# A hybrid decoder layer on one core: a fourth accumulator bank, gated operand loads, and one weight tile prepared earlier

## The chip, the cores and the metric

The kernel runs on one core of a Trainium2 chip. A core has TensorE (PE, matrix products, with its weight loads shown as PEld), VectorE (DVE), ScalarE (ACT), GpSimd (POOL) and SyncE (SP, here the queue that issues most transfers). The metric is device time in microseconds (us) of one launch, lower is better. "x3" behind a row stands for three instructions, L1631 for line 1631 of the kernel before.

## The reference

One layer of a decoder with four mixers side by side, for one prompt of 1024 positions and 8 samples of 8 positions (1088 tokens in all), model width 1024, in fp32:

```python
h = rmsnorm(x, norm_mix_pre[l])
(a_b, a_c, a_u, b_p, c_q, c_f, c_i, c_g, d_a, d_g) = jnp.split(h @ w_in[l], N_BLOCKS, axis=-1)
... # four mixers: ya, yb, yc, yd, 256 columns each
mix = jnp.concatenate([ya, yb, yc, yd], axis=-1) @ w_out[l]
x = x + rmsnorm(mix, norm_mix_post[l])
h = rmsnorm(x, norm_ffn_pre[l])
ff = (jax.nn.silu(h @ w_gate[l]) * (h @ w_up[l])) @ w_down[l]
x = x + rmsnorm(ff, norm_ffn_post[l])
```

The hidden width of the last part is 2816, 22 blocks of 128. The change touches how the products with `w_out`, with `w_gate` and `w_up`, and with `w_down` are fed; it changes none of them.

## The kernel before

Everything lies transposed: 128 features on the partitions, tokens along a row. Each fp32 operand is kept as two parts, a high one that ACT makes by a cast (CAST) and a low one that DVE makes by a subtract (`TT`, line 65, prints as TENSOR_TENSOR). A product is then three matmuls: high x high, high x low, low x high. So each weight tile needs a load, a cast and a subtract before PE can use all of it: `split2k` does the last two for a tile of 128x512.

The stages in order of time in the profiled execution:

1. to 335 us: norm of the input, the product with `w_in` (L997) in units of 128 columns, and the mixers between them. A planner (`hook`, `fill`, `drive`) gives DVE and PE their order here: at each group of matmuls it takes steps from three lists, `first`, `crit` and, when these have nothing, `bulk`. Their order on these two engines is then the order in which they were written. The last two units are 14 and 15; behind unit 15 a gate (`c_g`) multiplies the results `ys[4]` and `ys[5]` by silu(z).
2. 335 to 440 us: `project`, the product with `w_out` (L1131). Its right operands are the high and low parts `XH[k]`, `XL[k]` of the mixers' results, made by `put_y` in the order `korder` = (6, 7, 2, 3, 0, 1, 4, 5), and PE goes through k in that order. Its weights are `WO[n]`, for each of 8 output tiles two half tiles, h = 0 for k of 0 to 3 and h = 1 for k of 4 to 7. `out_steps` loads, casts and subtracts one `WO[n]`.
3. 440 to 925 us: the hidden units. Most go through `strassen(i, pr)` (L1403, from 518 us): two blocks of tokens and two of hidden features with 7 products of 12 matmuls each in place of 8. `pr` counts two pairs of token pieces, and `together` runs both in step: one product of pr 0, one of pr 1. The 7 products go into PSUM banks: b11 into a; t2 into b; t1 into c; b21 onto a; t3 onto b; t4 onto b; b22 onto c. Between them DVE reads sums out of the banks. PSUM has 8 banks, and the two in step use 6.
4. 925 to 1094 us: the down projection `down2` (L1631), again 7 products a step, in 4 groups g of 4 steps j. The right operands of group g are 14 tiles of 128x1088, from DRAM (`hx`): for g = 0 loaded and split on the chip, for the others loaded ready by POOL's queue (`x_item`, 42 loads). Free places for them are kept in `room`: 23 places, of which 14 are in use by a group; in the last step of a group each product frees two. `xs.step()` takes the next load in hand. The sums go to `acc` and `accp`; ACT copies (L1642, L1651) or DVE adds.
5. to 1181 us: the rest of the down projection (L1513), the last norm and the output.

From `down2` on the orders of PE, DVE, ACT and POOL are those in which the instructions are written. In stage 3 a scheduler orders them.

Of the kernel before, what the change touches and what calls it, by code (L numbers as in the profile page):

```python
# [17 lines left out]
P = 128  # L18
# [34 lines left out]
def body(ctx, tc, xn, xT, win, wout, wgu, wdn, par, con, msk, poolw, s_conv, s_pool, s_hgrn, s_conf,  # L53
# [330 lines left out]
    def chain(*gens):  # L384
        for g in gens:
            yield from g
# [636 lines left out]
    def out_steps(pools):  # L1023
        n = len(WO)
        WO.append([wop(pools) for h in range(2)])
        raws = [raw2k() for h in range(2)]
        for h in range(2):
            SY.dma_start(raws[h].rearrange("p (k c) -> p k c", c=P), wout[n][:, h * 4:h * 4 + 4])
        for h in range(2):
            yield 0.6  # L1030
            split2k(raws[h], WO[n][h])

# [16 lines left out]
    with tc.manual_schedule(engines={mybir.EngineType.PE, mybir.EngineType.DVE}):  # L1049
        for i, n in enumerate(UNITS):  # L1050
            handler, j = HANDLERS[n]
            nxt = UNITS[i + 1] if i + 1 < len(UNITS) else None
            if n in pu:
                first.append(handler(j, pu[n]))
                if i == 1:
                    until(lambda: free["mm"] >= 3)
                continue
            until(lambda: n in wq and len(wq[n]) == 2 and free["mm"] >= 3)
            give(mm=-3)
            ps = mm3()  # L1060
            if nxt is not None:
                load_unit(nxt)
                first.append(chain(wait(3), prep_steps(nxt)))
            else:
                bulk.insert(0, put_y())
            drive(unit(n, ps))
            del wq[n]
            first.append(handler(j, ps))
        bulk.insert(0, chain(out_steps([(wp, 4)]), out_steps([(wp, 4)])))
        until(lambda: not first and not crit and not bulk)  # L1070
    ph1.close()
    ph12.close()
# [315 lines left out]
    quads = {}  # L1388

    def strassen(i, pr):  # L1390
        a, b, c = bank(), bank(), bank()
        if i >= 2 * NPAIR:
            hst = T(w3, [P, 2, PW], "hst", bufs=2)
        else:
            if i % 2 == 0:
                quads[pr] = T(px, [P, 4, PW], "x")
            hst = quads[pr][:, 2 * (i % 2):2 * (i % 2) + 2]

        def prod(ps, wop, name, first):
            x = xop(name, pr)  # L1400
            for kk in range(4):
                for wi, xi in ((0, 0), (0, 1), (1, 0)):
                    PE.matmul(ps[:, :PW], wop[:, wi, kk * P:(kk + 1) * P], x(kk, xi),  # L1403
                              start=first and kk == 0 and wi == 0 and xi == 0, stop=kk == 3 and wi == 1,
                              skip_group_check=True)

        def buf(tag):
            return T(w3, [P, PW], tag, bufs=2)

        a11, s2, s1, a12, s3, a22, s4 = hid[i]  # L1410
        prod(a, a11, "b11", True)
        p1 = buf("p1")
        S.copy(p1, a[:, :PW])
        yield
        prod(b, s2, "t2", True)
        u2 = buf("u2")
        TT(u2, b[:, :PW], p1, ALU.add)
        yield
        prod(c, s1, "t1", True)
        yield  # L1420
        prod(a, a12, "b21", False)
        g0 = buf("g0")
        S.activation(g0, a[:, :PW], AF.Silu)
        yield
        prod(b, s3, "t3", False)
        c22 = buf("c22")
        TT(c22, b[:, :PW], p1, ALU.add)
        TT(c22, c[:, :PW], c22, ALU.add)
        yield
        prod(b, a22, "t4", False)  # L1430
        TT(p1, b[:, :PW], p1, ALU.add)
        yield
        prod(c, s4, "b22", False)
        TT(u2, c[:, :PW], u2, ALU.add)
        S.activation(u2, u2, AF.Silu)
        oa, ob = PIECES[2 * pr], PIECES[2 * pr + 1]
        TT(hst[:, 0], g0, p1)
        TT(hst[:, 1], u2, c22)
        if i >= 2 * NPAIR:
            SY.dma_start(hd[i][:, oa:oa + PW], hst[:, 0])  # L1440
            SY.dma_start(hd[i][:, ob:ob + PW], hst[:, 1])
        elif i % 2:
            pair_sums(i // 2, pr)
        yield
# [96 lines left out]
    def x_item(g, e):  # L1541

        p, name = 2 * g + e % 2, OPS[e // 2]
        src = hx[p][OPS.index(name)]

        def begin():
            if g:
                return None
            raw = T(w4, [P, 2 * PW], "raw", bufs=3).rearrange("p (q c) -> p q c", c=PW)
            SY.dma_start(raw, src[:, :2 * PW].rearrange("p (q c) -> p q c", c=PW))  # L1550
            return raw

        def work(raw):
            i, t = take()
            if g:
                GP.dma_start(t, src.bitcast(F32R))
            t = t.rearrange("p (w q c) -> p w q c", w=2, q=2)
            if not g:
                S.copy(t[:, 0], raw)
                TT(t[:, 1], raw, f32(t[:, 0]), ALU.subtract, eng=V if e % 2 else GP)  # L1560
            xop2[p, name] = t, i

        return begin, work

    def h_items(k):

        def item(c):
            o, n = DC[c]

            def begin():  # L1570
                raw = T(w4, [P, 2 * PW], "raw", bufs=3)[:, :n]
                SY.dma_start(raw, hd[k][:, o:o + n])
                return raw

            def work(raw):
                if c == 0:
                    hops[k] = [take()[1] for _ in range(2)]
                hi, lo = (h[:, o:o + n] for h in hops[k])
                S.copy(hi, raw)
                TT(lo, raw, f32(hi), ALU.subtract, eng=GP)  # L1580

            return begin, work

        return [item(c) for c in range(len(DC))]


    def load_ws(g, j):
# [35 lines left out]
    def down2(g, j, pr, ws, accp):  # L1623
        a, b, c = bank(), bank(), bank()
        oa, ob = PIECES[2 * pr], PIECES[2 * pr + 1]

        def prod(ps, name, first):
            for q in range(2):
                x = xop2[2 * g + q, name][0]
                for wi, xi in ((0, 0), (0, 1), (1, 0)):  # L1630
                    PE.matmul(ps[:, :PW], ws[name][wi][q], x[:, xi, pr], start=first and q == 0 and wi == 0 and xi == 0,  # L1631
                              stop=q == 1 and wi == 1, skip_group_check=True)

        def add(jj, o, ps):
            y = acc[jj][:, o:o + PW]
            TT(y, ps[:, :PW], y, ALU.add)

        y = accp[pr][:, j]
        prod(a, "b11", True)
        yield  # L1640
        if g == 0:
            S.copy(y, a[:, :PW])  # L1642
        else:
            TT(y, a[:, :PW], y, ALU.add)
        for ps, name, first, jj, o in ((b, "t2", True, j, ob), (c, "t1", True, j + NQ, ob), (a, "b21", False, j, oa),
                                       (b, "t3", False, j + NQ, ob), (c, "b22", False, j, ob), (b, "t4", False, j + NQ, oa)):
            prod(ps, name, first)
            yield
            y = acc[jj][:, o:o + PW]
            if g == 0 and name not in ("t3", "b22"):  # L1650
                S.copy(y, ps[:, :PW])  # L1651
            else:
                TT(y, ps[:, :PW], y, ALU.add)
# [41 lines left out]
    with tc.manual_schedule(engines={mybir.EngineType.Activation, mybir.EngineType.DVE, mybir.EngineType.PE, mybir.EngineType.Pool}):  # L1695
        for i, (g, j) in enumerate(order):
            wst.step()
            gens = [down2(g, j, pr, wsp[i], accp) for pr in range(2)]
            for e in range(8):
                for gen in gens:  # L1700
                    next(gen, None)
                if j == NQ - 1 and e < 7:
                    room += [xop2[2 * g + q, OPS[e]][1] for q in range(2)]
                if prep:
                    next(prep[0], None)
                if i == 0 and e < 2:
                    xs.step()
                elif i > 0 and e % 2 == 0 or j == NQ - 1 and e > 2:
                    if room and (xs.items or xs.raws):
                        xs.step()  # L1710
                if g == NGP - 1:
                    if e % 2 and (room[1:] or len(hs.items) % 3 != 1):
                        hs.step()
                    if e == 7:
                        add_p1(j + NQ, 0, GP if j < NQ - 1 else V)
                if i == len(order) - 1 and e in (0, 4, 1, 5):
                    if e < 4:
                        wraw.append(start_wd(e, 0))
                    else:
                        wds[e - 4, 0] = split_wd(e - 4, wraw.pop(0), (wp, 4) if e > 4 else None)  # L1720
            del prep[:]
# [165 lines left out]
```

## Time and profile before

| | us |
|---|---|
| median of three runs | 1183.06 (1183.0 to 1186.05) |
| profiled execution | 1182.58 |
| its span | 1180.8 |
| PE busy | 1145.0 (97%) |
| DVE busy | 881.4 (75%) |
| ACT busy | 455.5 (39%) |
| POOL busy | 96.8 (8%) |
| mean granted clock of PE | 0.995 |

The span goes from the first to the last instruction; the launch takes 1.78 us more. A row of a timeline gives start, duration, engine, line, operation, output<-inputs, and in brackets how long the engine was idle before and what ended that. A row of a table of waits gives who waited for whom, us in all, how often, and the longest. Granted clock is PE's share of its full speed.

### The profile page before, as it was taken

Reading aid. Unit: us, or ns where it says so; the run is one execution under the profiler, and the core shown is the slowest. Engines: PE = TensorE matmul, PEld = TensorE weight load, DVE = VectorE, ACT = ScalarE, POOL = GpSimd, SP = SyncE. Lnnn points to the kernel's source line nnn. Section 1 sums busy time; section 2 is a strip of 40 time slices with the busy share of each in tenths; the row PEclk is TensorE's granted clock in tenths of the full one; section 3 lists DMA queues with packets and bytes.
Section 4 is the critical chain, followed back from the end, with each engine's and each line's share of the span. In section 5 each row is a group of like instructions: output and inputs, shape, how many; then the busy total and the mean of one; then the engine's idle time right before and its main releaser. Section 6 shows DMA issues by size and latency. Waiting matters only on the chain.

```text
span 1180.8 us, 21827 instructions
## 1 busy us (share of the span) xinstructions
PE 1145.0 (97%) x8480; PEld 1111.1 (94%) x8480; DVE 881.4 (75%) x1831; ACT 455.5 (39%) x1006; POOL 96.8 (8%) x132
## 2 busy tenths in 40 slices
PE   5999999999999999999999999999999999999995
PEld 4899899998999999999999999999999999999995
DVE  5478979997674678786667787787676568888676
ACT  7535322253364453442333444444343442123321
POOL 2000000000000000000000000000000320127323
PEclk9999999999999999999999999999999999999998
DMA  7011112211145123022331542453454965843555
GB/s 264 30 42 24 37 38 69 41 37 29 41 157 176 39 75 129 24 80 79 112 112 50 186 162 95 162 170 111 140 182 125 297 207 180 298 159 105 168 101 105
DMA packets 103401, 136.91 MB, mean 116 GB/s; under 512 B 25025, under 2 KB 72257, under 8 KB 103297
## 3 DMA queue, kind: packets, MB, share of 16 engines
q1 hardware_dynamic: 94944, 108.71, 29.3%
q0 software_dynamic: 8352, 26.81, 7.8%
q8 instruction: 66, 1.08, 0.4%
q14 instruction: 39, 0.31, 0.1%
HBM read 94.90 MB, written 40.57 MB: 115 GB/s over the span
## 4 chain that ended last, share of the span: by engine, by line
PE 84%; DVE 5%; DMA 4%; issue 2%; ACT 2%; POOL 1%; SPq 0%; DVEq 0%; ACTq 0%; POOLq 0%
PE p L1403 27%; PE mm L997 16%; PE p L1631 14%; PE p L1131 8%; PE p L1513 6%; PE p L1312 5%; PE mm L148 2%; PE sm L811 1%; DVE wop L65 1%; DMA raw<-wgu 1%; DMA hx<-hi 1%; DVE raw L65 1%; DMA y<-xn 1%; DMA raw<-hx 1%; PE sm L886 1%
## 5 line engine op out<-in xcount | busy, mean ns | idle before, releaser
L65 DVE TENSOR_TENSOR wop<-raw,wop 128x512 fp32r<-128x512 f32 (+2 forms) x296 | 196.1, 675 | 105.3 <-ACT wop L1020 95.0
L1020 ACT CAST wop<-raw 128x512 fp32r<-128x512 f32 (+1 forms) x240 | 142.5, 604 | 252.0 <-DVE raw L65 115.7
L1403 PE MATMUL p<-xh,wop 128*128 128x272 f32 x1216 | 235.1, 288 | 0.0
L1403 PEld LDWEIGHTS p<-xh,wop 128*128 128x128 f32 x1216 | 193.3, 188 | 0.0
L1403 PE MATMUL p<-t,wop 128*128 128x272 f32 x912 | 179.3, 288 | 5.2 <-DVE c L65 5.2
L1403 PE MATMUL p<-xl,wop 128*128 128x272 f32 x608 | 175.6, 289 | 0.0
L997 PE MATMUL mm<-xh,wop 128*128 128x256 f32 (+2 forms) x864 | 175.3, 331 | 0.0
L1403 PEld LDWEIGHTS p<-t,wop 128*128 128x128 f32 x912 | 145.6, 188 | 6.5 <-DVE c L65 6.5
L997 PEld LDWEIGHTS mm<-xh,wop 128*128 128x128 f32 x864 | 137.4, 188 | 6.0 <-issue 1.1
L1403 PE MATMUL p<-x,wop 128*128 128x272 f32 x456 | 131.0, 287 | 0.0
L1403 PEld LDWEIGHTS p<-xl,wop 128*128 128x128 f32 x608 | 114.4, 188 | 0.0
L1131 PE MATMUL p<-xh,wop 128*128 128x272 f32 x512 | 100.6, 293 | 2.0 <-DVE wop L65 2.0
L997 PE MATMUL mm<-xl,wop 128*128 128x256 f32 (+2 forms) x432 | 97.3, 333 | 0.0
L1403 PEld LDWEIGHTS p<-x,wop 128*128 128x128 f32 x456 | 86.0, 189 | 0.0
L1131 PEld LDWEIGHTS p<-xh,wop 128*128 128x128 f32 x512 | 82.2, 191 | 2.2 <-DVE wop L65 2.2
L1631 PE MATMUL p<-xh,wop 128*128 128x272 f32 x456 | 81.6, 287 | 1.1 <-ACT x L1642 1.1
L1631 PE MATMUL p<-xl,wop 128*128 128x272 f32 x456 | 81.0, 287 | 0.0
L65 DVE TENSOR_TENSOR raw<-raw,raw 128x512 f32<-128x512 f32 (+1 forms) x123 | 71.2, 589 | 9.6 <-DMA raw<-wgu 8.1
L71 DVE SCALAR_TENSOR_TENSOR y<-u,taps,y 128x1024 f32<-128x1024 f32 x60 | 77.0, 1284 | 1.6
L1131 PE MATMUL p<-xl,wop 128*128 128x272 f32 x256 | 74.5, 291 | 0.0
L1312 PE MATMUL p<-xh,wop 128*128 128x272 f32 x384 | 74.1, 289 | 0.0
L997 PEld LDWEIGHTS mm<-xl,wop 128*128 128x128 f32 x432 | 69.2, 188 | 3.3 <-issue 0.8
(322 smaller groups left out, 1972.9 us busy)
## 6 DMA issues: line engine op xcount, KB each, us to landing
raw<-wgu SPq DMA_DIRECT2D x88, 256.0 KB, 3.0
hx<-hi SPq DMA_DIRECT2D x84, 136.0 KB, 2.1
raw<-win SPq DMA_DIRECT2D x40, 256.0 KB, 2.9
hx<-x SPq DMA_DIRECT2D x64, 136.0 KB, 2.5
raw<-wdn SPq DMA_DIRECT2D x32, 256.0 KB, 3.8
xh<-hx POOLq DMA_DIRECT2D x15, 544.0 KB, 9.8
xl<-hx POOLq DMA_DIRECT2D x15, 544.0 KB, 10.7
x<-hx POOLq DMA_DIRECT2D x12, 544.0 KB, 9.7
```

The costliest lines, as they stand in the source:

```text
L65: (eng or V).tensor_tensor(out, a, b, op)
L71: (eng or V).scalar_tensor_tensor(out=out, in0=a, scalar=s, in1=b, op0=op0, op1=op1)
L148: PE.matmul(ps[c][:, :n], hl[:, wi, kk], X[k][:, o:o + n], start=k == 0 and wi == 0 and X is XH, stop=k == KT - 1 and wi == 1)
L811: PE.matmul(ps[:rows, g * P:(g + 1) * P], kk[:, o:o + rows], qz[hf][:, :, g * 64:(g + 1) * 64], start=True, stop=True, skip_group_check=True)
L886: PE.matmul(op[hs, :gn], v[:gn, g, hs], attn[:gn, g, h, :gn], start=True, stop=g == 0, skip_group_check=True)
L997: PE.matmul(ps[c][:, :w], hl[:, wi, kk], X[k][:, o:o + w], start=k == order[0] and wi == 0 and X is XH, stop=k == order[-1] and wi == 1)
L1020: S.copy(hl[:, 0], raw)
L1131: PE.matmul(ps[nt][:, :PW], WO[nt][k // 4][:, wi, kk:kk + P], X[k][:, o:o + PW], start=k == korder[0] and wi == 0 and X is XH, stop=k == k ...
L1312: PE.matmul(ps[r][:, :PW], w[:, wi, (k % 4) * P:(k % 4 + 1) * P], X[k][:, o:o + PW], start=k == 0 and wi == 0 and X is XH, stop=k == KT - ...
L1403: PE.matmul(ps[:, :PW], wop[:, wi, kk * P:(kk + 1) * P], x(kk, xi), start=first and kk == 0 and wi == 0 and xi == 0, stop=kk == 3 and wi == 1,
L1513: PE.matmul(ps[:, :n], wd[:, wi, kk * P:(kk + 1) * P], hops[k][xi][:, o:o + n], start=first and kk == 0 and wi == 0 and xi == 0, stop=not ...
L1631: PE.matmul(ps[:, :PW], ws[name][wi][q], x[:, xi, pr], start=first and q == 0 and wi == 0 and xi == 0, stop=q == 1 and wi == 1, skip_group ...
```

## The change

Three edits.

First, in `strassen`, a fourth bank d. The product t4 starts in d and no longer continues in b. The sums are regrouped: t3 and p1 from b go into p1, then c and p1 into c22, and later d and p1 into p1. There are three sums as before. All 8 banks are then in use.

```diff
-        a, b, c = bank(), bank(), bank()
+        a, b, c, d = (bank() for _ in range(4))
...
         prod(b, s3, "t3", False)
+        TT(p1, b[:, :PW], p1, ALU.add)
         c22 = buf("c22")
-        TT(c22, b[:, :PW], p1, ALU.add)
-        TT(c22, c[:, :PW], c22, ALU.add)
+        TT(c22, c[:, :PW], p1, ALU.add)
         yield
-        prod(b, a22, "t4", False)
-        TT(p1, b[:, :PW], p1, ALU.add)
+        prod(d, a22, "t4", True)
+        TT(p1, d[:, :PW], p1, ALU.add)
```

Second, in the down projection, each of the 42 ready loads is preceded on POOL by a one-column add that reads the sum written last (`mark`), so that the load isn't issued before that sum. Which products take a load in hand changes too: in steps 0 to 2 of a group products 0, 3 and 6 (with the very first step of all, products 3 and 6), where it was 0, 2, 4 and 6 (and none in the first step). In step 3 it is 0 and 2 to 7; before, in groups 1 to 3, the same.

```diff
             if g:
+                if mark:
+                    TT(gate1, mark[0], mark[0], ALU.add, eng=GP)
                 GP.dma_start(t, src.bitcast(F32R))
...
+    mark = []
+    gate1 = T(const, [P, 1], "gate")
...
             y = acc[jj][:, o:o + PW]
+            mark[:] = [y[:, :1]]
...
-                elif i > 0 and e % 2 == 0 or j == NQ - 1 and e > 2:
+                elif e % 3 == 0 if j < NQ - 1 else e != 1:
```

Third, `WO[0]` is prepared ahead of `put_y`, where it and `WO[1]` were prepared behind it; and each `WO[n]` is split with h = 1 first.

```diff
-        for h in range(2):
+        for h in (1, 0):
             yield 0.6
             split2k(raws[h], WO[n][h])
...
-                bulk.insert(0, put_y())
+                bulk.insert(0, chain(out_steps([(wp, 4)]), put_y()))
...
-        bulk.insert(0, chain(out_steps([(wp, 4)]), out_steps([(wp, 4)])))
+        bulk.insert(0, out_steps([(wp, 4)]))
```

DVE between the mixers and `project`, before. `wop` is a half tile of weights (3141 and 3142 are `WO[0]`, 3154 and 3155 `WO[1]`), `xl` a low part (20 and 21 are k = 6 and 7, 16 and 17 k = 2 and 3, 14 and 15 k = 0 and 1, 18 and 19 k = 4 and 5), `y_27` is the gated `ys[5]`.

```order
L65 TENSOR_TENSOR y_26_106<-y_26_106,z_3048 128x448
L65 TENSOR_TENSOR xl_20_94<-y_28_108,xh_12_86 128x1088
...
L65 TENSOR_TENSOR xl_15_89<-y_23_103,xh_7_81 128x1088
L65 TENSOR_TENSOR wop_3141<-raw_3143,wop_3141 128x512
L65 TENSOR_TENSOR y_27_107<-y_27_107,z_3137 128x256
L65 TENSOR_TENSOR y_27_107<-y_27_107,z_3137 128x384
L65 TENSOR_TENSOR y_27_107<-y_27_107,z_3137 128x448
L65 TENSOR_TENSOR wop_3142<-raw_3144,wop_3142 128x512
L65 TENSOR_TENSOR wop_3154<-raw_3156,wop_3154 128x512
L65 TENSOR_TENSOR wop_3155<-raw_3157,wop_3155 128x512
L65 TENSOR_TENSOR xl_18_92<-y_26_106,xh_10_84 128x1088
```

The same place after. 3053 and 3052 are now `WO[0]`, h = 1 and h = 0; 3152 and 3151 are `WO[1]`.

```order
L65 TENSOR_TENSOR y_26_106<-y_26_106,z_3048 128x448
L65 TENSOR_TENSOR wop_3053<-raw_3055,wop_3053 128x512
L65 TENSOR_TENSOR wop_3052<-raw_3054,wop_3052 128x512
L65 TENSOR_TENSOR xl_20_94<-y_28_108,xh_12_86 128x1088
...
L65 TENSOR_TENSOR xl_15_89<-y_23_103,xh_7_81 128x1088
L65 TENSOR_TENSOR wop_3152<-raw_3154,wop_3152 128x512
L65 TENSOR_TENSOR y_27_107<-y_27_107,z_3147 128x256
L65 TENSOR_TENSOR y_27_107<-y_27_107,z_3147 128x384
L65 TENSOR_TENSOR y_27_107<-y_27_107,z_3147 128x448
L65 TENSOR_TENSOR wop_3151<-raw_3153,wop_3151 128x512
L65 TENSOR_TENSOR xl_18_92<-y_26_106,xh_10_84 128x1088
```

Two subtracts moved from behind k = 1 and y to ahead of k = 6, and two in place of four now stand between y_26's low part (k = 4) and those before it.

DVE in the next-to-last hidden unit (about 896 us), before: `c` is c22, `p` on the right a bank (10015 is b and 10016 c of pr 0, 10033 and 10034 those of pr 1) or p1 (1278, 1283), `raw` and `wop` the next units' weights.

```order
L65 TENSOR_TENSOR c_1288_10142<-p_10015,p_1278_10030 128x272
L65 TENSOR_TENSOR raw_10257<-raw_10256,raw_10257 128x2x128
L65 TENSOR_TENSOR c_1288_10142<-p_10016,c_1288_10142 128x272
L65 TENSOR_TENSOR c_1289_10157<-p_10033,p_1283_10048 128x272
L65 TENSOR_TENSOR c_1289_10157<-p_10034,c_1289_10157 128x272
L65 TENSOR_TENSOR wop_10480<-raw_10256,wop_10480 128x512
L65 TENSOR_TENSOR p_1278_10030<-p_10015,p_1278_10030 128x272
```

After, at the same rows (10050, 10051 and 10052 are b, c and d of pr 0; 10069 and 10070 b and c of pr 1; 1314 and 1320 are p1):

```order
L65 TENSOR_TENSOR p_1314_10066<-p_10050,p_1314_10066 128x272
L65 TENSOR_TENSOR raw_10294<-raw_10293,raw_10294 128x2x128
L65 TENSOR_TENSOR c_1325_10180<-p_10051,p_1314_10066 128x272
L65 TENSOR_TENSOR p_1320_10085<-p_10069,p_1320_10085 128x272
L65 TENSOR_TENSOR c_1326_10195<-p_10070,p_1320_10085 128x272
L65 TENSOR_TENSOR wop_10519<-raw_10293,wop_10519 128x512
L65 TENSOR_TENSOR p_1314_10066<-p_10052,p_1314_10066 128x272
```

The sums stand where they stood; only t4's result is now read from a bank of its own (10052).

POOL at the start of the down projection, before: the last subtract of group 0's operands, and then loads alone.

```order
L65 TENSOR_TENSOR x_10583<-raw_10528,x_10583 128x544
L1556 DMA x_10714<-hx 128x1088
L1556 DMA xh_1384_10749<-hx 128x1088
L1556 DMA xl_1386_10784<-hx 128x1088
L1556 DMA xh_1388_10817<-hx 128x1088
```

After: a gate stands ahead of each load, and reads a column of the sum named behind the arrow.

```order
L65 TENSOR_TENSOR x_10622<-raw_10567,x_10622 128x544
L65 TENSOR_TENSOR gate_5421<-t_1_1390_10585 128x1
L1558 DMA x_10678<-hx 128x1088
L65 TENSOR_TENSOR gate_5421<-t_0_1386_10581 128x1
L1558 DMA xh_1412_10728<-hx 128x1088
L65 TENSOR_TENSOR gate_5421<-t_1_1390_10585 128x1
L1558 DMA xl_1423_10759<-hx 128x1088
```

The loads keep their order among themselves; each now stands behind a sum.

## The prediction, made before the changed kernel ran

> **What bounds the kernel now.** I read the page first (span, engines, the chain that ended last), then what TensorE (PE) waited for, then the timelines of the engines around the waits that the change touches, and the granted clock in those stretches.
>
> ```profile
> span 1180.8 us, 21827 instructions
> PE 1145.0 (97%) x8480; PEld 1111.1 (94%) x8480; DVE 881.4 (75%) x1831; ACT 455.5 (39%) x1006; POOL 96.8 (8%) x132
> PE 84%; DVE 5%; DMA 4%; issue 2%; ACT 2%; POOL 1%; SPq 0%; DVEq 0%; ACTq 0%; POOLq 0%
> ```
>
> PE is busy for 1145.0 of 1180.8 us and holds 84% of the chain. The change takes away no matmul, so all it can win is PE's idle time, and time in which PE ran below its full clock. The waits of PE, summed by line (us in total, times, longest):
>
> ```profile
> PE sm L249 <- DVE y L68: 10.6, 2, 10.4
> PE p L1403 <- DVE c L65: 5.2, 4, 2.6
> PE p L1131 <- DVE wop L65: 2.0, 1, 2.0
> PE mm L148 <- DVE xl L71: 1.5, 4, 0.9
> PE p L1631 <- ACT x L1642: 1.1, 1, 1.1
> ```
>
> The largest, L249, lies in the input norm, and no hunk touches it. The other three lines of the change's places are L1403 (hidden units), L1131 (w_out product) and L1631 (down projection): 5.2 + 2.0 + 1.1 = 8.3 us. Each hunk stands against one of them.
>
> **A. w_out weights ahead of the mixers' split.** PE, DVE and ACT (start, duration, wait before) at the start of L1131:
>
> ```profile
> 335.43 0.29 PE L1131 MATMUL p<-xl,wop 128*128 128x272 f32 x1
> 337.69 0.52 PE L1131 MATMUL p<-xh,wop 128*128 128x272 f32 x2 [1.97 <-DVE wop L65]
> 340.46 0.43 PE L1131 MATMUL p<-xl,wop 128*128 128x272 f32 x1
> 323.79 1.48 DVE L65 TENSOR_TENSOR y<-y,z 128x256 f32<-128x256 f32 x3 [1.69 <-ACT z L449]
> 326.41 1.29 DVE L65 TENSOR_TENSOR xl<-y,xh 128x1088 fp32r<-128x1088 f32 x1 [1.14 <-ACT xh L1043]
> 333.71 1.29 DVE L65 TENSOR_TENSOR xl<-y,xh 128x1088 fp32r<-128x1088 f32 x1 [0.18 <-ACT xh L1043]
> 334.92 0.69 DVE L65 TENSOR_TENSOR wop<-raw,wop 128x512 fp32r<-128x512 f32 x1
> 335.55 1.47 DVE L65 TENSOR_TENSOR y<-y,z 128x256 f32<-128x256 f32 x3
> 336.94 1.89 DVE L65 TENSOR_TENSOR wop<-raw,wop 128x512 fp32r<-128x512 f32 x3
> 338.75 2.69 DVE L65 TENSOR_TENSOR xl<-y,xh 128x1088 fp32r<-128x1088 f32 x5
> 324.45 0.63 ACT L1020 CAST wop<-raw 128x512 fp32r<-128x512 f32 x1
> ```
>
> PE starts its first product with the k = 6 pair of matmuls that need only the high part of the weights, then stops until DVE has the low part of that half tile: the first of the three subtracts from 336.94 ends near 337.57, and PE goes on at 337.69. In the new order both subtracts of WO[0] (0.63 us each, a third of the 1.89) stand behind the y at 323.79. They run from 325.27 to about 326.53, in DVE's 1.14 us gap before 326.41. The high part that the first subtract reads is cast well before; the second reads that of 324.45, ready at 325.08. The six XL subtracts behind them start 0.12 us late at most and catch up, since each waits for ACT in turn (0.18 us at 333.71). So the wait of 1.97 us goes.
>
> What is late next: the low part of k = 4, the first of the five at 338.75. Two of the four subtracts that stood before it are gone from there; one subtract of WO[1] stays before y (334.92 to 335.55), then y to 336.94, the other of WO[1] to 337.57, and k = 4's low part to 337.57 + 1.29 = 338.86 (before: 338.75 + 1.29 = 340.04). PE wants it as matmul 20 of the product, 19 after the start at 335.31: 335.31 + 19 x 0.125 = 337.69. So PE stalls there for about 1.15 us, and does this matmul at 338.9 where before it did it at 340.46: 1.56 us gained. A second part is in the clock (stretch, its length, PE busy with the number of matmuls, granted clock, DMA share, GB/s):
>
> ```profile
> 337.70:339.30 1.60, 1.60 (x12) 0.99 0.29 83
> 339.30:342.50 3.20, 3.20 (x16) 0.50 0.94 256
> 342.50:345.70 3.20, 3.20 (x26) 0.97 0.92 312
> 532.80:536.00 3.20, 1.59 (x14) 1.00 0.29 102
> 894.00:896.80 2.80, 0.24 (x3) 1.00 0.77 264
> ```
>
> From 339.3 to 342.5 PE had half its clock: 16 matmuls where 26 go at full clock, 3.2 us that hold 1.6 us of work. Of its loss, 0.58 us lies before 340.46 and is in the 1.56; another 1.02 us lies behind it and is won only if the slow stretch goes. It is the only such stretch of these, and it starts 1.6 us after the wait ends; I take it as owed to this wait, with the matching doubt that the waits at 534 and 894 (rows below) left the clock at 1.00. So A = 1.56 + 1.02 = 2.6 us. Bounds: 0.5 (a slow stretch of the same length stays, and the later weight tiles, whose casts come in another order, cost 0.5) and 2.0 + 1.6 = 3.6.
>
> The Trainium skill ("TensorE: Matmul & The Clock Gate", Part 1, The HAM clock gate) says that the clock is halved only after an idle window of about 3.4 us, and that this window runs free of the kernel. By that rule alone a 1.97 us gap would not be the cause, the slow stretch could stay, and A would be 1.0; the trace agrees with it at 894 (2.56 us idle, clock 1.00) and not here, unless another cause is at work. The rows decide for 2.6; the rule's case is rival 1.
>
> **B. A fourth bank for t4.** The hidden units' waits, and the DVE work they wait for:
>
> ```profile
> 535.95 0.39 PE L1403 MATMUL p<-t,wop 128*128 128x272 f32 x1 [1.61 <-DVE c L65]
> 893.87 0.29 PE L1403 MATMUL p<-t,wop 128*128 128x272 f32 x1
> 896.72 0.39 PE L1403 MATMUL p<-t,wop 128*128 128x272 f32 x1 [2.56 <-DVE c L65]
> 534.85 0.69 DVE L65 TENSOR_TENSOR raw<-raw,raw 128x512 f32<-128x512 f32 x1 [1.96 <-DMA raw<-wgu]
> 535.46 0.44 DVE L65 TENSOR_TENSOR c<-p,p 128x272 f32<-128x272 f32 x1
> 896.23 0.43 DVE L65 TENSOR_TENSOR c<-p,p 128x272 f32<-128x272 f32 x1
> 896.91 0.43 DVE L65 TENSOR_TENSOR c<-p,c 128x272 f32<-128x272 f32 x1
> ```
>
> t4 accumulates into bank b, which DVE's c22 sum must have read first; DVE stood behind preparation of the next weights (at 534.85 itself behind a load). t4 in its own bank waits for nothing here: the four waits, 5.2 us, go. The DVE work is the same three sums of 0.43 us. The bank is there: the two units in step used six of eight, now eight, and the next unit's first bank was read by ACT's silu several products before.
>
> Late next: b22 goes on in bank c, which the second sum must have read. It comes two products after t4 (t4 of both pairs, 24 matmuls x 0.125 = 3.0 us). At 896 PE would begin t4 at 894.0 and b22 at 897.0; the sum in c ends at 896.91 + 0.43 = 897.34, so some 0.3 us stays. At 535 the second sum stands behind the one at 535.46 and a weight subtract of 0.69 us, so it ends by 537.0, and b22 of that pair is wanted at 534.34 + 3.0 = 537.34: nothing. So B = 5.2 - 0.3 = 4.9; bounds 0 and 5.2.
>
> **C. Gated and paced operand loads.** 42 gates of one column on POOL, 42 loads moved behind them.
>
> ```profile
> 940.95 0.65 PE L1631 MATMUL p<-xh,wop 128*128 128x272 f32 x3 [1.12 <-ACT x L1642]
> 940.00 0.62 ACT L1020 CAST wop<-raw 128x512 fp32r<-128x512 f32 x1 [4.22 <-DMA raw<-wdn]
> 940.52 0.67 ACT L1642 COPY x<-p 128x272 f32<-128x272 f32 x2
> 933.88 1.94 SPq L1590 DMA_DIRECT2D raw<-wdn  x2
> 924.14 0.77 POOL L1556 DMA_DIRECT2D x<-hx  x1
> 931.06 0.53 POOL L1556 DMA_DIRECT2D xl<-hx  x1 [2.41 <-DMA x<-hx]
> 936.00:941.00 5.00, 3.88 (x32) 1.00 1.11 406
> raw<-wdn SPq DMA_DIRECT2D x32, 256.0 KB, 3.8
> xl<-hx POOLq DMA_DIRECT2D x15, 544.0 KB, 10.7
> ```
>
> PE's only wait here is for ACT's copy out of a bank, which stood behind a weight cast, which waited 4.22 us for raw<-wdn. That load was issued from 933.88 and landed near 940.0, over 6 us after, while nine operand loads of 544 KB, issued at 924 to 931, kept the DMA engines full (share 1.11, 406 GB/s). With the gates POOL no longer runs ahead: the loads come one for each three products, the first around 931. The weight load then has one or two of them beside it and should take its usual 3.8 us; landing near 938, its cast is done before the copy is due at about 939.5. So C = 1.1 us.
>
> The gate itself is 128x1 on an engine that is 8% busy. Behind it on POOL stand only loads, the splits of the first group (all issued ahead of the first gate) and in the last group adds and splits; a gate waits for a sum of the step just past. DVE's next sum into the same columns waits for the gate's read, a product or more later: I cost that at nothing, covered by DVE's 25% idle time. The risk is the loads: the last operands of the next group can start only as the group's last step frees their slots, at its fifth to sixth product, and are wanted 10 to 11.5 us later (a step is 84 matmuls x 0.125 = 10.5). Against 10.7 us, the landing in a burst of 9 to 14, that is between 0.7 us late and 0.8 early, at three group changes; with five in flight, and not 9 to 14, I estimate half that landing, well in time. Bounds of C: gain 1.1; loss 3 x 0.7 = 2.1, all of it if the landing stays that of a burst.
>
> **The sum.** -2.6 - 4.9 - 1.1 = -8.6 us against the profiled execution, 1182.58 us (span 1180.8 and 1.78 around it): 1174.0. The median of the runs shown is 0.48 above the profiled one, so 1174.5 us.
>
> **Rivals.**
>
> 1. The slow stretch isn't owed to the wait, or the new stall of 1.15 us brings it too: A = 1.56 less the 0.58 that the clock gave = 1.0. For it: longer waits left the clock alone. Against: it follows the only wait of that stage. 1174.5 + 1.6 = 1176.1.
> 2. The fourth bank only moves the wait: DVE, late for other reasons, makes b22 wait for c as t4 did for b. For it: DVE is late by its place behind weight preparation, which stays. Against: 3.0 us of slack where the longest wait was 2.56. With B = 0: 1179.4.
> 3. The paced loads land late and PE waits at each of the three group changes. For it: they were issued early and all at once, now late by rule. Against: fewer compete. In the mild form, a landing of 12 to 15 us, each change costs 1 to 4 us, 3 to 12 in all: 1177 to 1186.6. It ends slower than before by over 0.3% once it takes over 12.1 us, 4 at each change, a landing of 14 to 15.5 us in place of 10.7.
> 4. C isn't gained (the weight load is late for another reason): 1175.6.
>
> **How the numbers follow.** A measurement of this kernel tells about 0.3% (3.55 us) from no change, so faster is below 1179.5 and slower above 1186.6. The forecast has 0.54; rival 1 0.16; rival 4 0.10; rival 2 0.08, half of it under 1179.5; rival 3 0.12, of which 0.05 ends slower and 0.07 within. Faster: 0.54 + 0.16 + 0.10 + 0.04 = 0.84; within 0.04 + 0.07 = 0.11; slower 0.05. The range goes from 1171.5 (A 3.6, B 5.2, and 1.3 us from loads that no longer collide) to 1180.0 (rival 2 with 0.6 of lateness), and leaves out most of rival 3.
>
> **What would show it.** A: L1131's wait for wop gone, one of about 1.15 us for xl in its place near 337.7, no clock of 0.50 behind it. B: no wait of L1403 for c over 0.4 us. C: POOL's loads spread over the steps, no wait of L1631 for ACT, none for a load. Wrong: a clock of 0.50 anywhere in 338 to 346; waits of L1403's b22; waits of L1631 for xh, xl or x at the group changes.

## The result, and the profile after

| | before | after |
|---|---|---|
| median, us (runs) | 1184.45 (9) | 1178.70 (9) |
| lowest to highest | 1183.0 to 1189.62 | 1175.69 to 1179.39 |
| profiled execution | 1182.58 | 1176.22 |
| its span | 1180.8 | 1174.4 |

The ratio of after to before is 0.9942, 95% interval 0.9926 to 0.9957: 0.58% faster, some 6.9 us (the two medians differ by 5.75). The forecast was 8.6 us and a time of 1174.5, worked out from a median of 1183.06; the nine runs of before now have 1184.45. The nine times after fall into two groups: 1175.7 to 1176.7 us at a mean granted clock of 0.995, and 1178.7 to 1179.4 at 0.992 or 0.993; the profile is of the first group, the median is in the second.

The page after, and its waits of PE:

```profile
span 1174.4 us, 21922 instructions
PE 1144.4 (97%) x8480; PEld 1111.4 (95%) x8480; DVE 880.8 (75%) x1831; ACT 454.9 (39%) x1006; POOL 109.9 (9%) x174
PE 92%; DVE 3%; DMA 2%; ACT 2%; issue 1%; SPq 0%; POOL 0%; ACTq 0%; DVEq 0%; POOLq 0%
PE sm L249 <- DVE y L68: 10.5, 2, 10.3
PE mm L148 <- ACT xh L250: 2.1, 3, 1.5
PE p L1131 <- DVE xl L65: 1.0, 1, 1.0
PE p L1403 <- DVE c L65: 0.6, 1, 0.6
```

The waits of L1131 for wop (2.0 us), of L1403 (5.2) and of L1631 (1.1) are gone. In their place stand the two that the prediction named: 1.0 us for xl and one of 0.6 us for c. These are the places in the timeline, and POOL with its gates (L1631 of before is L1636 now, L1556 is L1558):

```profile
340.47 0.39 PE L1131 MATMUL p<-xl,wop 128*128 128x272 f32 x1 [1.02 <-DVE xl L65]
892.48 0.39 PE L1403 MATMUL p<-xh,wop 128*128 128x272 f32 x1 [0.59 <-DVE c L65]
891.99 0.43 DVE L65 TENSOR_TENSOR c<-p,p 128x272 f32<-128x272 f32 x1
922.39 0.19 POOL L65 TENSOR_TENSOR gate<-t 128x1 f32<-128x1 f32 x1 [5.38 <-ACT t L1657]
922.63 0.77 POOL L1558 DMA_DIRECT2D x<-hx  x1
926.47 0.18 POOL L65 TENSOR_TENSOR gate<-t 128x1 f32<-128x1 f32 x1 [3.06 <-DVE t L65]
926.92 0.58 POOL L1558 DMA_DIRECT2D xh<-hx  x1 [0.27 <-PE p L1636]
xl<-hx POOLq DMA_DIRECT2D x15, 544.0 KB, 5.2
x<-hx POOLq DMA_DIRECT2D x12, 544.0 KB, 5.0
928.00:933.00 5.00, 5.00 (x42) 1.00 0.87 267
```

The loads now come one by one and land after 5.0 to 5.2 us, where in bursts it was 9.7 to 10.7. The last row (stretch, PE busy, clock, DMA) lies 11 us into the down projection, as 936 to 941 does before: the DMA share is 0.87 at 267 GB/s in place of 1.11 at 406. A gate takes 0.2 us.

The weight load that the cast of L1020 stood behind lands earlier for two reasons, of which the prediction had one. Counted from the first matmul of the down projection, it was issued after 9.15 us and in flight for 6.09 before; after, it is issued after 4.41 us and in flight for 3.11. It is issued earlier mainly since SyncE, which issues it, waits less for the stores of the hidden units (hd), as its own waits between 912 and 946 us show, first before, then after:

```profile
SPq L1590 <- DMA hd<-hst: 7.4, 2, 6.3
...
SPq L1595 <- DMA hd<-hst: 2.8, 2, 2.2
```

So every wait went as forecast, and 2 us were missing. I followed the same matmul through both profiles (PE's order is the same). Lengths of the stages, from a stage's first matmul to its last, in us:

| | start to L1131 | L1131 | L1403 | L1631 | L1513 |
|---|---|---|---|---|---|
| before | 335.31 | 105.02 | 407.00 | 168.56 | 73.18 |
| after | 336.90 | 102.39 | 399.99 | 168.85 | 74.02 |

The product between L1131 and L1403 (L1312) is 0.1 us shorter and what follows L1513 0.55 us longer. The stage before L1131 is 1.6 us longer, though the change leaves PE's work there as it was; 0.9 us of that is there already at L997's first matmul (53.72 and 54.66 us), the rest grows within L997. L1631 is no shorter although it has lost its only wait, and L1513 is 0.8 us longer. The next view is of the matmuls of one line in a stretch (the number behind x): L997 from 60 to 200 us, and the down projection from 945 to 1085 us, first before, then after.

```profile
60.00:200.00 140.00, 116.69 (x673) 1.00 0.16 43
945.00:1085.00 140.00, 140.00 (x1127) 1.00 0.59 196
...
60.00:200.00 140.00, 116.68 (x670) 1.00 0.15 42
945.00:1085.00 140.00, 140.00 (x1116) 1.00 0.68 210
```

With PE busy all the time and the clock at 1.00, the down projection gets through 1116 matmuls after, where it was 1127. The matmuls follow each other more slowly. That was not in the prediction, and the experiments are about it.

### The profile page after: what moved, and what is told of

Read it like the earlier page. It is cut to its first block, busy times and chain, and to the rows that moved or that the text cites. A ratio compares the mean times of both kernels' runs of the same rounds, so it can differ in the third digit from the quotient of the medians.

```text
span 1174.4 us, 21922 instructions
## 1 busy us (share of the span) xinstructions
PE 1144.4 (97%) x8480; PEld 1111.4 (95%) x8480; DVE 880.8 (75%) x1831; ACT 454.9 (39%) x1006; POOL 109.9 (9%) x174
## 4 chain that ended last, share of the span: by engine, by line
PE 92%; DVE 3%; DMA 2%; ACT 2%; issue 1%; SPq 0%; POOL 0%; ACTq 0%; DVEq 0%; POOLq 0%
PE p L1403 31%; PE mm L997 18%; PE p L1636 14%; PE p L1131 8%; PE p L1513 6%; PE p L1312 6%; PE mm L148 2%; PE sm L811 2%; DMA y<-xn 1%; DMA hx<-hi 1%; DVE wop L65 1%; PE sm L886 1%; PE p L1097 1%; PE sm L898 0%; PE sm L409 0%
## 5 line engine op out<-in xcount | busy, mean ns | idle before, releaser
L1403 PE MATMUL p<-xh,wop 128*128 128x272 f32 x1216 | 235.2, 288 | 0.6 <-DVE c L65 0.6
L1020 ACT CAST wop<-raw 128x512 fp32r<-128x512 f32 (+1 forms) x240 | 142.0, 604 | 239.3 <-DVE raw L65 120.3
L1403 PEld LDWEIGHTS p<-xh,wop 128*128 128x128 f32 x1216 | 193.3, 188 | 0.8 <-DVE c L65 0.8
L1403 PE MATMUL p<-t,wop 128*128 128x272 f32 x912 | 176.8, 288 | 0.0
L997 PE MATMUL mm<-xh,wop 128*128 128x256 f32 (+2 forms) x864 | 175.9, 331 | 0.0
L1403 PE MATMUL p<-xl,wop 128*128 128x272 f32 x608 | 175.4, 288 | 0.0
L1403 PEld LDWEIGHTS p<-t,wop 128*128 128x128 f32 x912 | 145.3, 189 | 0.0
L997 PEld LDWEIGHTS mm<-xh,wop 128*128 128x128 f32 x864 | 137.9, 188 | 5.7 <-issue 1.1
L1403 PE MATMUL p<-x,wop 128*128 128x272 f32 x456 | 130.8, 287 | 0.0
L1403 PEld LDWEIGHTS p<-xl,wop 128*128 128x128 f32 x608 | 114.4, 188 | 0.0
L1131 PE MATMUL p<-xh,wop 128*128 128x272 f32 x512 | 98.9, 290 | 0.0
L997 PE MATMUL mm<-xl,wop 128*128 128x256 f32 (+2 forms) x432 | 97.5, 333 | 0.0
L1403 PEld LDWEIGHTS p<-x,wop 128*128 128x128 f32 x456 | 86.3, 189 | 0.0
L1636 PE MATMUL p<-xh,wop 128*128 128x272 f32 x456 | 82.2, 289 | 0.0
L1636 PE MATMUL p<-xl,wop 128*128 128x272 f32 x456 | 81.5, 288 | 0.0
L1131 PEld LDWEIGHTS p<-xh,wop 128*128 128x128 f32 x512 | 81.0, 188 | 0.0
L71 DVE SCALAR_TENSOR_TENSOR y<-u,taps,y 128x1024 f32<-128x1024 f32 x60 | 77.0, 1283 | 1.6
L1131 PE MATMUL p<-xl,wop 128*128 128x272 f32 x256 | 73.9, 289 | 1.0 <-DVE xl L65 1.0
L1312 PE MATMUL p<-xh,wop 128*128 128x272 f32 x384 | 74.0, 290 | 0.0
L65 DVE TENSOR_TENSOR t<-p,t 128x272 f32<-128x272 f32 (+3 forms) x138 | 60.6, 450 | 15.9 <-PE p L1636 8.2
```

Source lines behind the costliest of these rows:

```text
L65: (eng or V).tensor_tensor(out, a, b, op)
L71: (eng or V).scalar_tensor_tensor(out=out, in0=a, scalar=s, in1=b, op0=op0, op1=op1)
L997: PE.matmul(ps[c][:, :w], hl[:, wi, kk], X[k][:, o:o + w], start=k == order[0] and wi == 0 and X is XH, stop=k == order[-1] and wi == 1)
L1020: S.copy(hl[:, 0], raw)
L1131: PE.matmul(ps[nt][:, :PW], WO[nt][k // 4][:, wi, kk:kk + P], X[k][:, o:o + PW], start=k == korder[0] and wi == 0 and X is XH, stop=k == k ...
L1312: PE.matmul(ps[r][:, :PW], w[:, wi, (k % 4) * P:(k % 4 + 1) * P], X[k][:, o:o + PW], start=k == 0 and wi == 0 and X is XH, stop=k == KT - ...
```

## The experiments

All were timed against the kernel before, beside it on the same chip (1 to 4 on one chip, 5 to 8, 9 to 11 and 12 on three others). A ratio is turned into us with 1184. "Pace" is the mean time from one matmul's start to the next at a line, gaps over 0.215 us left out, worked out from the trace.

**1. The kernel before again.** No edit.

> The kernel before, unchanged, run as if it were an experiment: how far two profiles of one program differ. Theory W (the change wins the waits it names; what is missing from the predicted 8.6 us is scatter between executions): the matmuls of the down projection follow each other at any pace between 0.1245 and 0.1256 us, the project stage may start up to 1.6 us later than 335.31, and the mean granted clock differs from run to run between 0.992 and 0.995, with times some 3 us apart to match. Theory L (the gated loads cost what they win, by slowing the down projection's matmuls): the pace here is 0.1245 again, within 0.0003, and the start of project is within 0.3 us of 335.31.

Ratio 1.0006 (0.9992 to 1.0020). The paces are those of the first profile to 0.0001 us (L997 0.1653, L1403 0.1254, L1631 0.1245, L1513 0.1641), and L1131 starts at 335.66, 0.35 us later than in the first profile. So the pace is not scatter between executions; of the late start, a few tenths can be. What does differ is where the clock drops: the 0.50 stretch in L1131 is not there, though the wait of 2.0 us is, and there is another, which starts in a wait of 3.5 us in L1403 (stretch, PE busy, clock):

```profile
893.40:897.00 3.60, 0.20 (x2) 0.91 0.72 226
897.00:903.90 6.90, 6.84 (x33) 0.55 0.22 64
903.90:907.00 3.10, 3.10 (x27) 1.00 0.15 54
```

**2. The fourth bank alone.**

```diff
-        a, b, c = bank(), bank(), bank()
+        a, b, c, d = (bank() for _ in range(4))
...
-        prod(b, a22, "t4", False)
+        prod(d, a22, "t4", True)
```

(with its sums, as in the change.)

> The fourth bank alone. Theory W: the four waits of 5.2 us at L1403 become one of 0.3 to 0.7 us, the time falls by 4.5 to 5; the waits of L1131 (2.0) and L1631 (1.1) stay. Theory L says the same of this part. Rival (the wait only moves): waits of L1403 sum to over 2 us again, in b22, and the time falls by under 3.

Ratio 0.9964 (0.9951 to 0.9978). That is 4.3 us (2.6 to 5.8). L1403 keeps one wait of 0.2 us; the stage takes 400.60 us in place of 407.00. The waits of L1131 (2.0) and L1631 (1.3) stay.

**3. The w_out tile alone.**

```diff
-                bulk.insert(0, put_y())
+                bulk.insert(0, chain(out_steps([(wp, 4)]), put_y()))
```

(with the order of halves and the shorter chain behind.)

> The w_out tile ahead of the split alone. Theory W: L1131's wait for wop (2.0 us) gives way to one of 1.0 to 1.2 us for xl; with the stretch at half clock gone the time falls by 2.6 us. Rival (the slow stretch is not owed to this wait): a 3.4 us stretch at half clock stays in the records, there or elsewhere, and the time falls by 1.0.

Ratio 0.9981 (0.9963 to 0.9998): 2.2 us (0.2 to 4.4), which holds both 2.6 and the rival's 1.0. The wait for xl is 1.0 us, no clock under 1.00 in L1131, and the stage takes 102.57 us: 2.45 less than in the first profile of before, which had the 0.50 stretch, and 1.19 less than in experiment 1 (103.76), which had not.

**4. Gates and pacing alone.**

```diff
             if g:
+                if mark:
+                    TT(gate1, mark[0], mark[0], ALU.add, eng=GP)
                 GP.dma_start(t, src.bitcast(F32R))
...
+    gate1 = T(const, [P, 1], "gate")
...
-                elif i > 0 and e % 2 == 0 or j == NQ - 1 and e > 2:
+                elif e % 3 == 0 if j < NQ - 1 else e != 1:
```

> Gates and pacing of the operand loads alone. Theory W: the wait of 1.1 us at L1631 goes, no other comes, the time falls by 1.1 us, and the pace of the down projection's matmuls lies anywhere between 0.1245 and 0.1256 us. Theory L: the pace is 0.1256 us, as it was with the whole change, 1.5 us lost over 1344 matmuls, and the time is the same or up to 0.5 us longer than before.

Ratio 1.0025 (1.0008 to 1.0042): slower. The wait at L1631 is gone and no load is waited for, but the paces are those of the changed kernel, at L997 too (0.1664), some 600 us ahead of the first gate. So theory L doesn't hold as stated: a gate can't slow what runs long before it. What this kernel shares with the changed one, and not with experiments 1 to 3, is the gate's tile. It takes 32 bytes of each partition in the pool of constants, and the operands xh, xl and x, whose pools lie below on the same side, stand 32 bytes lower. So do the tiles of the norms' sums and most of the constants. The weight tiles stay, and so do the tiles t (high parts of the sums that t2, t3 and t4 multiply in L1403).

**5. The shift alone.**

```diff
     mhalf = T(const, [P, 1], "mhalf")
+    pad = T(const, [P, 1], "pad")
+    V.memset(pad, 0.0)
```

> The kernel before with one unused one-column tile more in the pool of constants (written once at the start): no gate, no pacing, no bank. In the loads kernel and in the whole change the gate's tile moved every tile behind it in that pool, the operands xh, xl and x among them, by 32 bytes, from addresses that are multiples of 64 to such as are 32 more; here the same shift stands alone. Theory S (the shift sets the pace of the matmuls): start to start 0.1676 us at L997 in place of 0.1666, 0.1256 at L1631 in place of 0.1245, 0.1666 at L1513 in place of 0.1645, 0.1251 at L1403 in place of 0.1254: 1.3 + 1.5 + 0.9 - 1.0 = 2.7 us slower than before, with the waits of before (5.2, 2.0, 1.1). Theory L (gates and pacing slow the matmuls): the paces and the time of before.

Ratio 1.0020 (1.0006 to 1.0035): 2.4 us slower (0.7 to 4.1), by a tile that nothing reads. Here only four of the constants move along with the operands. Paces 0.1665, 0.1251, 0.1256 and 0.1661: those of the changed kernel. The two stretches shown above:

```profile
60.00:200.00 140.00, 116.68 (x670) 1.00 0.15 42
945.00:1085.00 140.00, 140.00 (x1116) 1.00 0.59 198
```

**6. Gates and pacing, the gate's tile 64 bytes long.**

```diff
-    gate1 = T(const, [P, 1], "gate")
+    gate1 = T(const, [P, 16], "gate")[:, :1]
```

> Gates and pacing alone again, with the gate's tile made 64 bytes long, so that the operands stand at multiples of 64 as before. Theory S: paces of before (0.1666, 0.1245, 0.1645, 0.1254), no wait at L1631, 1.1 us faster than before. Theory L: 0.1256 at L1631, and 2 to 3 us slower than before, like the loads kernel without this.

Ratio 1.0042 (1.0027 to 1.0058). I had taken the shift to matter by the remainder of the address to 64. It doesn't: paces 0.1674, 0.1257, 0.1250 and 0.1666, a third set, slower still at L997, L1403 and L1513.

**7. The whole change with the 64-byte tile.** The same edit in the changed kernel.

> The whole change with the gate's tile 64 bytes long. Theory S: 2.7 us faster than the whole change as it was: ratio to before 0.9942 - 0.0023 = 0.9919, which is the predicted 8.6 us less some half-clock stretches. Theory L: no faster than the whole change, 0.994.

Ratio 0.9953 (0.9936 to 0.9970); the paces of experiment 6. The expectation rested on the same wrong remainder and missed; no gain over the change as it was.

**8. The same, with y's gating behind the low part of k = 4.**

```diff
+        if j == 1:
+            yield from after(("split", 4))
         for c, (o, n) in enumerate(CH):
             TT(ys[4 + j][:, o:o + n], ys[4 + j][:, o:o + n], z[:, o:o + n])
...
                 yield n * 0.0011
+            done.add(("split", k))
```

> The same, and the gating of ys[5] by silu(z) put behind the low part of k = 4 on DVE, which takes away what made project wait for xl (1.0 us). Both theories: that wait goes and nothing comes in its place, 1.0 us less than the kernel with the longer tile alone, ratio to before 0.991. If the low part of k = 5 comes late instead, a wait for xl of up to 1 us shows some 8 us into project and nothing is won.

Ratio 0.9956 (0.9940 to 0.9973): nothing won. DVE, and then PE (L1134 is L1131 of before):

```profile
340.04 0.69 DVE L65 TENSOR_TENSOR wop<-raw,wop 128x512 fp32r<-128x512 f32 x1 [1.32 <-ACT wop L1022]
340.65 1.28 DVE L65 TENSOR_TENSOR xl<-y,xh 128x1088 fp32r<-128x1088 f32 x1
341.99 0.39 PE L1134 MATMUL p<-xl,wop 128*128 128x272 f32 x1 [0.96 <-DVE xl L65]
345.66 0.52 PE L1134 MATMUL p<-xh,wop 128*128 128x272 f32 x2 [0.28 <-DVE wop L65]
```

The low part of k = 4 now stands behind a weight subtract whose cast ACT makes late, and DVE sits idle for 1.32 us; the wait for xl stays, and one for the next weights is added.

**9. The whole change, no tile moved.** The gate writes into a tile of the norms that is out of use by then.

```diff
-    gate1 = T(const, [P, 1], "gate")
+    gate1 = T(const, [P, 3], "rs_b1a")[:, :1]
```

> The whole change, with the gate writing into a tile of the norms that is no longer used, so that no tile moves and xh, xl and x stand where they stood before. Theory S (address sets the pace): paces of before, 0.1653 us start to start at L997, 0.1254 at L1403, 0.1245 at L1631, 0.1641 at L1513; 2.6 us less than the whole change as it was, ratio to before 0.992. A rival (the gated loads themselves slow the last stages): pace at L1631 0.125 or more and a ratio of 0.994 or more.

Median 1174.30 us, ratio 0.9920 (0.9903 to 0.9937), the lowest median of all kernels here (its interval overlaps those of the changed kernel and of experiment 10). Paces 0.1654, 0.1254, 0.1245 and 0.1635, and the numbers of the two stretches are those of before again (1128 for 1127):

```profile
60.00:200.00 140.00, 116.69 (x673) 1.00 0.16 43
945.00:1085.00 140.00, 140.00 (x1128) 1.00 0.68 210
```

No wait at L1403 or L1631 is left; L1131 keeps its 1.0 us for xl.

**10. Bank and w_out tile, no gates and no pacing.** Edits 2 and 3.

> Bank and w_out tile, no gates and no pacing, addresses of before. Theory S: the wait of 1.1 to 1.4 us at L1631 is there; 1.2 us more than the kernel above, ratio to before 0.993. Rival (gates and pacing win nothing): the same time as the kernel above, within 0.5 us.

Ratio 0.9939 (0.9920 to 0.9958). The wait for ACT is there, and L1631 takes 169.10 us where experiment 9 took 167.14. The medians (1176.59 and 1174.30) agree with that, but the intervals overlap.

```profile
PE p L1631 <- ACT x L1642: 1.7, 1, 1.7
```

**11. A gate tile of 96 bytes,** `T(const, [P, 24], "gate")[:, :1]` in the changed kernel.

> The whole change with a gate tile of 96 bytes. So far the paces at L997, L1403, L1631 and L1513 were 0.1653, 0.1254, 0.1245, 0.1641 with the operands where they stood, 0.1664, 0.1251, 0.1256, 0.1661 moved by 32 bytes, 0.1674, 0.1257, 0.1250, 0.1666 moved by 64. If the pace goes by the address alone, in steps of 32 bytes and with a period of 128, this is a fourth set of four numbers, the same to 0.0002 in any kernel of this shift; if it goes by multiples of 64, it is the set of 32.

Ratio 0.9965 (0.9949 to 0.9981); paces 0.1673, 0.1257, 0.1256 and 0.1662. It is not the set of 32. With one kernel at this shift, that the set is the same in any other wasn't tried.

**12. Gates and pacing alone, no tile moved.** Edit 4 with the tile of edit 9.

> Gates and pacing alone, with the gate writing into a tile no longer used, so that no tile moves. Theory S: paces of before, no wait at L1631, 1.1 to 1.5 us less than before, ratio 0.9988, where the same edit with a tile of its own gave 1.0025 (moved by 32 bytes) and 1.0042 (by 64). Theory L (the gated loads themselves cost): 1.001 or more.

Ratio 0.9995 (0.9977 to 1.0013). Paces of before, no wait at L1631, L1631 167.14 us where before had 168.56. The interval holds both 0.9988 and 1.001, so the time doesn't tell them apart; the stage does: 1.4 us shorter. Gates and pacing were not tried one without the other. The same edit gave 1.0025 with 32 bytes moved and 1.0042 with 64.

The paces by shift, in us, and what they cost against the first profile of before, from the counts of matmuls (1296, 3192, 1344 and 432; L1131 and L1312, left out, change by at most 0.3 us each). It is an estimate: where PE also waits, a part of it is hidden (L997: 1.4 us by the pace, 0.7 longer between the two profiles).

| operands moved by | L997 | L1403 | L1631 | L1513 | cost, us | kernels |
|---|---|---|---|---|---|---|
| 0 | 0.1653 to 0.1655 | 0.1254 | 0.1245 | 0.1634 to 0.1641 | 0 | before, 1, 2, 3, 9, 10, 12 |
| 32 bytes | 0.1664 to 0.1665 | 0.1251 | 0.1256 | 0.1661 | 2.7 | after, 4, 5 |
| 64 bytes | 0.1673 to 0.1674 | 0.1257 | 0.1250 | 0.1666 | 5.4 | 6, 7, 8 |
| 96 bytes | 0.1673 | 0.1257 | 0.1256 | 0.1662 | 5.8 | 11 |

The whole change at the four shifts measured 0.9920, 0.9942, 0.9953 and 0.9965 of before: 2.6, 3.9 and 5.3 us behind the first, in the order of the table, though the intervals of neighbours overlap.

## Why the prediction was right, and where it was short

The direction and the range held. By its steps:

**A (forecast 2.6 us).** The wait for wop went, the stall of 1.15 us for xl came with 1.02, and the stage lost 105.02 - 102.39 = 2.6 us between the two profiles. But 1.26 us of that is luck of the first profile: before, it took 105.02 with the 0.50 stretch and 103.76 without. Seven profiles here have the wait of 2.0 us, and the clock drops behind it in three of them (before, 2 and 4); seven don't have it, and it drops there in none. Three of seven against none of seven could still be chance. But between 320 and 1160 us the 14 profiles have five stretches at half clock in all (here, in 1, 2, 4 and 5), and each starts in a wait of 1.96 us or longer, or within 1.6 us of its end; of waits of 1.9 us or longer there are twelve, and seven brought none. So the stretch does hang on a wait, but not each time: 1.2 us always, and 1.26 more in 3 of 7 profiles. In the other four the gain is near rival 1's 1.0. The Trainium skill ("TensorE: Matmul & The Clock Gate", Part 1, The HAM clock gate) explains a drop by an activity window of about 3.4 us that runs free of the kernel. The traces agree in that these stretches are about 3.4 or 6.8 us long and come and go for the same code; they differ in that a stretch followed a wait of 1.96 or 1.97 us three times.

**B (forecast 4.9 us).** The waits went, and 0.59 us came at b22 of pr 0 near 892, where 0.3 was worked out. Against the first profile the term was still too small: the stage lost 7.0 us, 1.0 of it by the faster pace of 0.1251, and in experiment 9, without that, 6.9. I had summed PE's idle time. What a wait costs is the gap from start to start over the normal 0.125 us: matmuls overlap (each shows some 0.29 us, and they start 0.125 apart), and the first one behind a wait doesn't. At 896.72 the idle time is 2.56 us and the start comes 2.85 after the one before; the next is again 0.23 later. Over L1403 of before these gaps, with two short ones that the table of waits does not list under this line, come to 6.8 us. So for this profile 5.2 should have been 6.8. Two others without the bank and without a shift have less to lose: the stage takes 405.89 us in experiment 3 and 406.19 in 12, and with the bank 400.13 to 400.99, which makes B 4.9 to 6.9; and the time of experiment 2, 4.3 us (2.6 to 5.8), holds the forecast and not 6.8. These waits differ from execution to execution, so in part that is luck of the first profile too. Rival 2 fell.

**C (forecast 1.1 us).** The wait went, the weight load no longer meets a burst and is issued 4.7 us earlier besides, which the prediction didn't see (experiment 10, without gates and pacing, issues it after 9.71 us and has it in flight for 6.08; 9, with them, 4.97 and 2.81), and landing of the operands fell to half as estimated: L1631 1.4 us shorter in experiment 12 and 2.0 in 9 against 10. No load came late; rival 3 and rival 4 fell. The step that failed is "The gate itself is 128x1 on an engine that is 8% busy", which costs the gate as an instruction. Its tile moved the operands by 32 bytes, and by the paces PE lost 2.7 us net over four stages, three of which have no gate (experiment 5, the shift alone, measured 2.4). With that the hunk is 1.0025 by itself: as it was written, it costs more than it wins.

**The sum.** What the profiles give for the waits is A 1.2 to 2.4, B 4.9 to 6.9 and C 1.4 to 2.0: 7.5 to 11.3 us; kernel 9 is 9.5 below before (0.0080 x 1184, 7.5 to 11.5 by the interval), and the changed kernel's 6.9 (5.1 to 8.8) fits that less the shift's 2.4 to 2.7. The three parts timed alone, 4.3, 2.2 and 0.6, come to 7.1, with wide intervals. So the waits were worth about what was forecast, within these bounds, and what is missing is the shift, which was put at nothing. The low end of the range, 1171.5, doesn't come out of the three terms named beside it (3.6, 5.2 and 1.3 give 1173.0); with C's 1.1 it is 1171.9. That the median after was 1178.7 and not 1176 may have to do with one more stretch. In 7 of the 14 profiles here (2, 5, 6, 9, 10, 11 and 12), PE had half its clock for some 6.8 us near 307, where L997 alternates with 128x1 and 128x2 matmuls. The profile of before, and then of kernel 9:

```profile
307.40:314.20 6.80, 6.80 (x41) 1.00 0.01 4
...
307.40:314.20 6.80, 6.80 (x25) 0.53 0.02 6
```

The same matmul starts 0.1 us earlier in kernel 9 at 226 us, and 3.0 us later at 313. Two groups of times 3 us apart, at clocks 0.995 and 0.992, fit that; that the changed kernel's slower group had it there is not shown, since its one trace is of the other group.

## What to carry to other kernels

A wait costs the gap from start to start less the normal one: add what the pipelining loses (0.26 to 0.27 us for each wait of L1403 in the first profile, the gap behind it included) to the idle time that a table shows. A new tile, however small, can have a price of its own if it moves the operands of the bounding engine: put it where nothing moves, and if a stage that the change doesn't touch gets another pace, compare addresses before anything else. And split a change before believing its sum: here a tile of 32 bytes took back about a quarter of what the change without it wins (2.6 of 9.5 us by the two ratios), while every wait in the profile said that its part helped.

## What was unexpected in the hardware

The pace of 128x128 by 128x272 matmuls at full clock went from 0.1245 to 0.1256 us, and that of L997 from 0.1653 to 0.1674, with the place of the right operands in steps of 32 bytes, alike to 0.0002 us in all kernels of a shift (at L1513 to 0.0007). The lines don't agree on which shift is best: L1403 is fastest moved by 32, L997, L1631 and L1513 where they stood. Nor is it the place of a matmul's own operand alone. From a matmul's start to the next in L1403, those that read xh and xl, which moved, kept 0.125 and 0.126 us at 0, 32 and 64 bytes; those that read t, which didn't move, went from 0.1254 to 0.1256 us to 0.1250 at 32 bytes and 0.1268 at 64, and those that read x, which alternate with them, from 0.1252 to 0.1240 and 0.1249. Why, the runs don't say; only four places were tried, with the weights standing still. The Trainium skill ("SBUF — State Buffer", Operand start alignment) asks only that an operand starts at a multiple of its element's size, and says that its measurements timed nothing; no run here contradicts it, but speed does depend on the place.
